# First mixer of a diffusion trunk: weights' low parts by adding DMAs, the out projection in halves, 9 convolution taps a step

## The chip, the core and the metric

The kernel runs on one core of a Trainium2 chip as a single program. The metric is the time of the device in microseconds (us), measured around the whole program; the kernel before has a median of 1498.23 us of three runs (1498.07 to 1499.12). The core has TensorE (matmul), VectorE (DVE in the profile), ScalarE (ACT), GpSimd (POOL) and SyncE (SP), which here only issues the DMAs of the weights. All engines run their own instruction lists in order and wait for each other by semaphores.

## What is computed

A trunk of two layers works on 384 tokens (256 latent, 128 context) of 1024 channels, in float32. Each layer is a half-step SwiGLU FFN, a mixer and another half-step FFN, each behind an RMS norm with shift, scale and gate from a condition vector. The mixer of layer 0 is the one that is changed. Cut to what matters, it is:

```
cq, ckv, kr, u = split(h @ w_in)                 # 384, 256, 32 and 1024 columns
q   = rms_norm(cq) @ w_qu ;  k, v = from rms_norm(ckv) @ w_kvu and kr
attn = softmax(q k^T / sqrt(96)) v               # 8 heads, 512 channels together
a, b = split(u)
g = depthwise_conv(a * sigmoid(b), w_dw) + b_dw  # 31 taps, 512 channels
g = silu(layer_norm(g) * g_ln + b_ln)            # the layer-norm goes over the 512 channels
out = concat([attn, g]) @ w_out                  # 1024 -> 1024
x = x + gate * out
```

## The kernel before

Everything is held transposed: channels on the 128 partitions, tokens along the free dimension. A float32 matmul is done as three matmuls of a rounded type (float32r): each operand is split into a high part (the value rounded) and a low part (the value minus its high part), and `mm3` (line 263; its three matmuls are lines 265 to 267) adds low x high, high x low and high x high into one bank of PSUM. Activations are split as they are made. Weights are split as they are used: `Step` is one tile of weights (128 x up to 2048 columns, 1 MB) with the work that uses it, and `stream` runs a list of steps. It loads raw tiles through a ring of three buffers on SP's queue, splits the tiles of this step and the next (`split`, line 193; its cast is line 202, its subtraction line 203: for each half of 1024 columns ScalarE casts to `whi`, VectorE subtracts to `wlo`; four buffers of each kind), calls the step's matmuls (`mm`), and the step's `post` after the next split. A raw buffer is loaded again when both halves are split.

The program's order is not an engine's order. The framework's planner orders each engine's list when the program is built: of what is ready by its own estimates, the earliest in the program goes first, so later work that is ready fills gaps. Semaphore waits hold the actual order to the data.

The mixer of layer 0 (`mixer_a`) has ten steps: seven tiles of `w_in` (`in_unit`, 48 matmuls of 386 columns each, in the order ORD), then query weights, key/value weights, query weights. Behind every tile that completes a group of 128 convolution channels, `taps` puts 31 taps of that group into background queues (`self.bg`); a tap is one multiply-add of VectorE over 128 x 399 (line 859; the first of each group is line 856). After each step's `post`, `pop_bg(BG1)` issues BG1 = 6 of them, alternating between two queues. Attention runs in four groups of two heads: scores of the next group, transposes and products of this one (`pv`), softmax of the next, and then `pop_bg(BG2)` with BG2 = 8. After the attention `pop_bg(1000)` issues all taps that are left. `conv_ln` makes the layer-norm over the 512 channels: sums over channels by matmuls with a matrix of constants (line 937), centring and squares, their sums (line 951), a reciprocal root by small VectorE steps, its broadcast by matmuls (line 437), then scaling, SiLU and the split into channels 4 to 7 of MXh and MXl. The out projection (`out_steps`) has four steps of 48 matmuls; each makes two of the eight output blocks from all eight channels, the attention's 0 to 3 and the convolution's 4 to 7. `mixer_a` ends with these lines:

```
rest(MXh, MXl)
self.Hh, self.Hl = self.take_h(F32R)
self.pop_bg(1000)
self.conv_ln(ub, acc, MXh, MXl)
self.stream(self.out_steps(a["woa"], MXh, MXl, lambda: self.mods[l, GM], nxt))
```

Of the kernel before, what the change touches and what calls it, by code (L numbers as in the profile page):

```python
# [43 lines left out]
LATE = 400  # L44

ORD = (0, 1, 4, 5, 2, 6, 3)
BG1, BG2 = 6, 8

V_GF1, V_GMIX, V_GF2, V_GFIN, V_BMOD, V_C = 0, 16, 32, 48, 56, 200
V_GQL, V_GKVL, V_BDW, V_GLN, V_BLN, V_WDW, V_GQH, V_GKH = 216, 219, 221, 225, 229, 233, 357, 358  # L50
# [9 lines left out]
def pair_col(i, k):  # L60

    return (k // 4 * 8 + i * 4 + k % 4) * P


class Step:
    def __init__(self, ap=None, cols=0, split=True, mm=None, post=None, ring="raw"):
        self.ap, self.cols, self.split, self.mm, self.post, self.ring = ap, cols, split, mm, post, ring
        self.raw = self.buf = None
        self.parts = []
        self.pos = 1000  # L70
        self.then = None
# [8 lines left out]
class Trunk:  # L80
# [79 lines left out]
    def stream(self, steps):  # L160
        depth = {"raw": NRAW, "rawm": NRAWM}
        lead = sorted([s for s in steps if s.ap is not None and s.pos < 1000], key=lambda s: s.pos)
        rest = {r: deque(s for s in steps if s.ap is not None and s.ring == r and s.pos == 1000) for r in depth}
        out = {r: deque() for r in depth}

        def load():
            def one(s):
                if len(out[s.ring]) == depth[s.ring]:
                    return False
                pool = self.rawp if s.ring == "raw" else self.ffnp  # L170
                s.raw = pool.tile([P, UN], F32, tag=s.ring, name=s.ring, bufs=depth[s.ring])
                self.nc.sync.dma_start(out=s.raw[:, :s.cols], in_=s.ap)
                out[s.ring].append(s)
                if s.then:
                    s.then()
                return True

            while lead and one(lead[0]):
                lead.pop(0)
            if lead:  # L180
                return
            for r in ("raw", "rawm"):
                if r == "rawm" and i + 4 < mod1:
                    continue
                while rest[r] and one(rest[r][0]):
                    rest[r].popleft()

        i = 0
        mod1 = min([k for k, s in enumerate(steps) if s.ring == "rawm" and s.pos == 1000], default=0)
        load()  # L190
        done_split = set()

        def split(s):
            half = UN // 2 if s.cols == UN else (s.cols // P + 1) // 2 * P
            for c0, c1 in ((0, half), (half, s.cols)):
                n = c1 - c0
                if s.buf:
                    hi, lo = (b[:, c0:c1] for b in s.buf)
                else:
                    hi, lo = (self.splitp.tile([P, UN // 2], F32R, tag=t, name="w" + t)[:, :n] for t in ("hi", "lo"))  # L200
                raw = s.raw[:, c0:c1]
                self.nc.scalar.copy(hi, raw)  # L202
                self.nc.vector.tensor_tensor(out=lo, in0=raw, in1=hi.bitcast(F32), op=ALU.subtract)  # L203
                s.parts.append((c0, c1, hi, lo))
            done_split.add(id(s))

        consumed = set()

        def retire():
            for q in out.values():  # L210
                while q and id(q[0]) in consumed:
                    q.popleft()
            load()

        lead0 = any(s.buf for s in steps)
        prev = None
        for i, s in enumerate(steps):
            want = 0
            for x in steps[i:]:
                if x.ap is not None and x.split:  # L220
                    if id(x) not in done_split:
                        if x.raw is None:
                            break
                        split(x)
                        consumed.add(id(x))
                        retire()
                    want += 1
                    if want == (3 if i < NLEAD and lead0 else 2):
                        break
            if prev is not None and prev.post:  # L230
                prev.post()
            if s.mm:
                s.mm(s)
            while self.mid:
                self.mid.pop(0)()
            if s.ap is not None and not s.split:
                consumed.add(id(s))
            retire()
            due, self.later = self.later, []
            for f in due:  # L240
                f()
            prev = s
        if prev is not None and prev.post:
            prev.post()
        while self.later:
            due, self.later = self.later, []
            for f in due:
                f()
# [315 lines left out]
            self.stream(steps)  # L564


    def in_unit(self, ap, posts, get=None, before=None, after=None):

        st = {}

        def mm(s):
            if before:
                before()
            ps = [(get or self.ps_mm)() for _ in posts]
            st["p"] = ps
            for k in range(ND):
                for i, p in enumerate(ps):
                    self.mm3(p[:, :TB], *s.w(pair_col(i, k)), self.Hh[:, k], self.Hl[:, k],
                             k == 0, k == ND - 1)
                if k == 4:  # L580
                    self.pop_mid()

            if after:
                after()

        def post():
            for f, p in zip(posts, st["p"]):
                f(p)

        return Step(ap, UN, True, mm, post)  # L590

    def norm_in(self, ps, out):

# [121 lines left out]
    def out_steps(self, w, MXh, MXl, gate, nxt):  # L715
# [17 lines left out]

        return [step(u) for u in range(ND // 2)]


    def mixer_a(self, l, nxt):
        nc, a, tc = self.nc, self.a, self.tc
        with tc.tile_pool(name="ma", bufs=1, reuse_waits="tile") as mp:
# [7 lines left out]
            with tc.tile_pool(name="map", bufs=1, reuse_waits="tile") as pp:  # L747
# [116 lines left out]
                def q_step(u):  # L864
# [4 lines left out]
                                self.mm3(p[:, :T], *s.w((3 * h + k) * P), cqh[:, k], cql[:, k], k == 0, k == 2)  # L869
                            nc.vector.tensor_tensor(out=qT[4 * u + h], in0=p[:, :T], in1=ropeq[:, h % 2], op=ALU.mult)  # L870

                    return Step(a["wqu"][u], 1536, True, mm)

                def kv_step():
                    st = {}
# [14 lines left out]
                                         k == 0, k == 1)  # L890
                            nc.scalar.copy(Vt[:, kt], p)

                    return Step(a["wkvu"], UN, True, mm)

                heads = []
                for h in range(8):
# [5 lines left out]
                def bg(s):  # L902
                    post = s.post

                    def f():
                        if post:
# [2 lines left out]
                    s.post = f  # L909
                    return s  # L910

                steps = [self.in_unit(w[j], [p_ua(j), p_ub(j)]) for j in range(4)]
                steps += [self.in_unit(w[4], [p_ckv(0), p_ckv(1)]),
                          self.in_unit(w[5], [p_kr, p_cq(0)]),
                          self.in_unit(w[6], [p_cq(1), p_cq(2)])]
                steps = [steps[i] for i in ORD]
                steps += [q_step(0), kv_step(), q_step(1)]
                self.stream([bg(s) for s in steps])
            with tc.tile_pool(name="maa", bufs=1, reuse_waits="tile") as ap:
# [2 lines left out]
                rest(MXh, MXl)  # L922
                self.Hh, self.Hl = self.take_h(F32R)
                self.pop_bg(1000)
                self.conv_ln(ub, acc, MXh, MXl)
                self.stream(self.out_steps(a["woa"], MXh, MXl, lambda: self.mods[l, GM], nxt))

    def conv_ln(self, ub, acc, MXh, MXl):
        nc = self.nc
        cols = ((0, TL), (271, 399))  # L930
        n = self.tb("sq", 399)
        nc.vector.tensor_tensor(out=n, in0=acc[0], in1=acc[1], op=ALU.add)
        some = [n, acc[2], acc[3]]
        p = self.ps_ax()
        for o, (c0, c1) in ((0, cols[0]), (TL, cols[1])):
            for j in range(3):
                nc.tensor.matmul(p[:, o:o + c1 - c0], lhsT=self.ones, rhs=some[j][:, c0:c1], start=(j == 0), stop=(j == 2))
        sq = []
        for j in range(4):
            for o, (c0, c1) in ((0, cols[0]), (TL, cols[1])):  # L940
                nc.vector.scalar_tensor_tensor(out=acc[j][:, c0:c1], in0=p[:, o:o + c1 - c0], scalar=-2.0,
                                               in1=acc[j][:, c0:c1], op0=ALU.mult, op1=ALU.add)
            s = ub[j][:, 0:399]
            nc.scalar.activation(s, acc[j], AF.Square)
            sq.append(s)
            if j % 2:
                nc.vector.tensor_tensor(out=sq[j - 1], in0=sq[j - 1], in1=s, op=ALU.add)
        p = self.ps_ax()
        for t, c in enumerate((0, P, 271)):
            for j in (0, 2):  # L950
                nc.tensor.matmul(p[:, t:t + 1], lhsT=sq[j][:, c:c + P], rhs=self.one, start=(j == 0), stop=(j == 2))
        r3 = self.tb("r3", 3)
        self.rsqrt(r3, p[:, 0:3], 1.0 / 512)
        nc.scalar.activation(self.tb("ba", 2), r3[:, 0:2], AF.Silu)
        r = self.spread(None, r3)
        for j in range(4):
            n = self.tb("ta")
            for o, (c0, c1) in ((0, cols[0]), (TL, cols[1])):
                nc.vector.tensor_tensor(out=n[:, o:o + c1 - c0], in0=acc[j][:, c0:c1], in1=r[:, o:o + c1 - c0],
                                        op=ALU.mult)  # L960
            g = self.tb("g")
            nc.scalar.activation(g, n, AF.Silu, scale=self.v(V_GLN + j), bias=self.v(V_BLN + j))
            self.split_to(MXh[:, 4 + j], MXl[:, 4 + j], g)


    def mixer_c(self, l, nxt):
# [286 lines left out]
```

## Time and profile before

| | |
|---|---|
| median of three runs | 1498.23 us |
| the profiled execution | 1496.57 us, span 1494.8 us |
| TensorE busy | 1441.5 us (96%) |
| VectorE busy | 1209.1 us (81%) |
| ScalarE busy | 641.1 us (43%) |
| DMA queues, all | 248.36 MB, mean 166 GB/s |

The span runs from the first to the last instruction. Times in the trace are microseconds from its start. Matmuls overlap, so the duration of one is longer than the step from one to the next. The first mixer lies between 309 and 497 us.

### The profile page before, as it was taken

To read this page: it belongs to the slowest core of one execution; us is meant where nothing else is said; L and a number is where in the kernel's file an instruction comes from. 1 tells how busy PE (TensorE), PEld (TensorE's weight loads), DVE (VectorE), ACT (ScalarE), POOL (GpSimd) and SP (SyncE) were. 2 spreads that over 40 slices of the span, in tenths; PEclk is the share of its full clock that TensorE was granted. 3 is DMA by queue.
4 is the path that set the end of the run, shared out by engine and by line. 5 is a ranking of instruction groups with operands and counts; after the bars stand their busy time and mean duration, and the time that the engine had idled before them with its cause. 6 is when DMAs were issued, how large, how long until landed. Compare 5 with 4: busy or idle time off the path is not lost.

```text
span 1494.8 us, 21749 instructions
## 1 busy us (share of the span) xinstructions
PE 1441.5 (96%) x8274; PEld 1397.9 (94%) x8274; DVE 1209.1 (81%) x2544; ACT 641.1 (43%) x1143; POOL 1.8 (0%) x8
## 2 busy tenths in 40 slices
PE   7999999999938999999999999999999999999997
PEld 5999999999827999999999999999985899999997
DVE  6999999979997999999959998544799689555443
ACT  4433443346633543333334333333477553433332
POOL 0000000000000000000000000000000000000000
PEclk8999999999978999999999999999999999999999
DMA  8656557643102566656655664243420155332331
GB/s 360 253 205 228 215 210 233 233 164 103 57 1 88 222 220 231 225 193 224 241 218 196 221 230 150 89 136 134 162 85 29 57 201 194 113 134 95 116 123 56
DMA packets 40168, 248.36 MB, mean 166 GB/s; under 512 B 4448, under 2 KB 6272, under 8 KB 16384
## 3 DMA queue, kind: packets, MB, share of 16 engines
q1 hardware_dynamic: 37728, 245.04, 45.5%
q10 hardware_dynamic: 2336, 1.94, 0.4%
q8 instruction: 65, 1.06, 0.3%
q14 instruction: 39, 0.32, 0.1%
HBM read 244.98 MB, written 1.98 MB: 165 GB/s over the span
## 4 chain that ended last, share of the span: by engine, by line
PE 94%; DVE 3%; ACT 2%; DMA 1%; issue 1%; SPq 0%; DVEq 0%; ACTq 0%
PE ps_mm L265 28%; PE ps_mm L266 28%; PE ps_mm L267 28%; PE ps_mm L637 2%; PE ps_ax L687 2%; DVE acc L859 1%; PE ps_tr L267 1%; PE ps_tr L265 1%; PE ps_tr L266 1%; DMA raw<-wm 1%; PE ps_tr L679 1%; PE ps_tr L675 0%; ACT pr L656 0%; PE ps_ax L288 0%; PE ps_ax L437 0%
## 5 line engine op out<-in xcount | busy, mean ns | idle before, releaser
L202 ACT CAST whi<-raw 128x1024 fp32r<-128x1024 f32 (+1 forms) x348 | 330.1, 950 | 647.7 <-PE ps_mm L267 566.4
L265 PE MATMUL ps_mm<-Hh,wlo 128*128 128x386 f32 x1568 | 533.0, 341 | 4.8 <-DVE wlo L203 3.9
L266 PE MATMUL ps_mm<-Hl,whi 128*128 128x386 f32 x1568 | 532.0, 339 | 0.6 <-DVE Hl L392 0.6
L267 PE MATMUL ps_mm<-Hh,whi 128*128 128x386 f32 x1568 | 530.9, 339 | 0.0
L203 DVE TENSOR_TENSOR wlo<-raw,whi 128x1024 fp32r<-128x1024 f32 (+1 forms) x348 | 381.8, 1098 | 164.5 <-ACT whi L202 162.1
L265 PEld LDWEIGHTS ps_mm<-Hh,wlo 128*128 128x128 f32 x1568 | 295.9, 189 | 7.4 <-DVE wlo L203 4.4
L266 PEld LDWEIGHTS ps_mm<-Hl,whi 128*128 128x128 f32 x1568 | 296.7, 189 | 2.1 <-DVE Hl L392 1.1
L267 PEld LDWEIGHTS ps_mm<-Hh,whi 128*128 128x128 f32 x1568 | 295.7, 189 | 0.0
L266 PE MATMUL ps_mm<-Gl,whi 128*128 128x384 f32 x704 | 236.7, 336 | 0.0
L265 PE MATMUL ps_mm<-Gh,wlo 128*128 128x384 f32 x704 | 236.7, 336 | 0.0
L267 PE MATMUL ps_mm<-Gh,whi 128*128 128x384 f32 x704 | 236.7, 336 | 0.0
L368 DVE SCALAR_TENSOR_TENSOR junk<-rawm,eb 128x1024 bf16<-128x1024 f32 x130 | 158.5, 1219 | 1.0 <-ACT eb L143 1.0
L368 DVE SCALAR_TENSOR_TENSOR rawm<-rawm,eb 128x1024 f32<-128x1024 f32 x130 | 158.5, 1219 | 0.3
L265 PEld LDWEIGHTS ps_mm<-Gh,wlo 128*128 128x128 f32 x704 | 132.0, 187 | 0.0
L267 PEld LDWEIGHTS ps_mm<-Gh,whi 128*128 128x128 f32 x704 | 132.0, 187 | 0.0
L266 PEld LDWEIGHTS ps_mm<-Gl,whi 128*128 128x128 f32 x704 | 132.0, 187 | 0.0
L519 ACT CAST Gh<-g 128x384 fp32r<-128x384 f32 x88 | 45.0, 512 | 84.9 <-DVE g L516 84.6
L509 ACT ACTIVATE sa<-ta,ba 128x256 f32<-128x256 f32 (+1 forms) x176 | 70.3, 447 | 5.2 <-DVE ta L506 5.0
L859 DVE SCALAR_TENSOR_TENSOR acc<-ub,vec,acc 128x399 f32<-128x399 f32 x120 | 69.8, 630 | 0.0
L516 DVE SCALAR_TENSOR_TENSOR g<-t,bb,sa 128x256 f32<-128x256 f32 (+1 forms) x176 | 65.3, 412 | 0.8 <-ACT sa L509 0.8
L520 DVE TENSOR_TENSOR Gl<-g,Gh 128x384 fp32r<-128x384 f32 x88 | 48.9, 555 | 12.2 <-ACT Gh L519 12.2
L460 DVE SCALAR_TENSOR_TENSOR X<-ps_mm,mod,X 128x256 f32<-128x256 f32 x88 | 32.5, 412 | 30.4 <-PE ps_mm L267 30.4
(270 smaller groups left out, 1240.5 us busy)
## 6 DMA issues: line engine op xcount, KB each, us to landing
raw<-wi SPq DMA_DIRECT2D x86, 1024.0 KB, 4.8
rawm<-wmt SPq DMA_DIRECT2D x64, 1024.0 KB, 4.8
raw<-wo SPq DMA_DIRECT2D x64, 704.0 KB, 4.1
raw<-wia SPq DMA_DIRECT2D x7, 1024.0 KB, 4.7
raw<-wm SPq DMA_DIRECT2D x6, 1024.0 KB, 8.9
raw<-wic SPq DMA_DIRECT2D x6, 1024.0 KB, 4.8
raw<-woa SPq DMA_DIRECT2D x4, 1024.0 KB, 4.8
raw<-woc SPq DMA_DIRECT2D x4, 1024.0 KB, 4.8
```

The lines of the kernel that those rows point to most:

```text
L202: self.nc.scalar.copy(hi, raw)
L203: self.nc.vector.tensor_tensor(out=lo, in0=raw, in1=hi.bitcast(F32), op=ALU.subtract)
L265: mm(out, lhsT=lo, rhs=rh, start=start, stop=False)
L266: mm(out, lhsT=hi, rhs=rl, start=False, stop=False)
L267: mm(out, lhsT=hi, rhs=rh, start=False, stop=stop)
L368: self.nc.vector.scalar_tensor_tensor(out=junk, in0=raw[:, i], scalar=1.0, in1=self.eb[:, c], op0=ALU.mult, op1=ALU.mult, accum_out=out[:, ...
L460: nc.vector.scalar_tensor_tensor(out=self.X[:, d, s0:s1], in0=ps[:, s0:s1], scalar=gate[:, d, c:c + 1], in1=self.X[:, d, s0:s1], op0=ALU.m ...
L509: nc.scalar.activation(sa[:, s0:s1], ta[:, s0:s1], AF.Silu, bias=ba[:, c:c + 1])
L516: nc.vector.scalar_tensor_tensor(out=g[:, s0:s1], in0=t2[:, s0:s1], scalar=bb[:, c:c + 1], in1=sa[:, s0:s1], op0=ALU.add, op1=ALU.mult)
L519: nc.scalar.copy(Gh[:, f], g)
L520: nc.vector.tensor_tensor(out=Gl[:, f], in0=g, in1=Gh[:, f].bitcast(F32), op=ALU.subtract)
L859: nc.vector.scalar_tensor_tensor(out=acc[j], in0=src(t), scalar=w(t), in1=acc[j], op0=ALU.mult, op1=ALU.add)
```

## The change

The subtraction that makes a weight's low part is replaced, for all weights of the first mixer, by a negated copy on ScalarE (which rounds, so it is the negative high part) and a DMA from GpSimd's queue that adds the raw weight to it in SBUF:

```diff
                 raw = s.raw[:, c0:c1]
                 self.nc.scalar.copy(hi, raw)
-                self.nc.vector.tensor_tensor(out=lo, in0=raw, in1=hi.bitcast(F32), op=ALU.subtract)
+                if s.add:
+                    self.nc.scalar.activation(lo, raw, AF.Copy, scale=-1.0)
+                    self.nc.gpsimd.dma_start(out=lo.bitcast(F32), in_=raw, accum_op=ALU.add)
+                else:
+                    self.nc.vector.tensor_tensor(out=lo, in0=raw, in1=hi.bitcast(F32), op=ALU.subtract)
```

A step of 1024 columns is split in one piece. Nine taps are issued after every step and every attention group:

```diff
-BG1, BG2 = 6, 8
+BG1, BG2 = 9, 9
```

The out projection's first three steps are cut into a half for channels 0 to 3 and a half for channels 4 to 7, which add into the same banks of PSUM; each half loads its own 512 KB. The layer-norm becomes three parts that stand between the first halves, and `last` is the fourth step, whole:

```diff
+    def out_halves(self, w, MXh, MXl, gate, nxt):
+        half = UN // 2
+        sts = [{} for _ in range(3)]
+        def step(u, h):
+            st = sts[u]
+            def mm(s):
+                if h == 0:
+                    get = self.ps_tr if u == 2 else self.ps_mm
+                    st["p"] = [get(), get()]
+                for k in range(4 * h, 4 * h + 4):
+                    for i, p in enumerate(st["p"]):
+                        self.mm3(p[:, :T], *s.w(pair_col(i, k) - h * half), MXh[:, k], MXl[:, k],
+                                 k == 0, k == ND - 1)
...
+            return Step(w[u][:, h * half:h * half + half], half, True, mm, post if h else None, add=True)
+        last = self.out_steps(w, MXh, MXl, gate, nxt)[3]
+        last.add = True
+        return [step(u, 0) for u in range(3)], [step(u, 1) for u in range(3)], last
...
-                self.conv_ln(ub, acc, MXh, MXl)
-                self.stream(self.out_steps(a["woa"], MXh, MXl, lambda: self.mods[l, GM], nxt))
+                ln = [Step(mm=lambda s, f=f: f()) for f in self.conv_ln(ub, acc, MXh, MXl)]
+                first, second, last = self.out_halves(a["woa"], MXh, MXl, lambda: self.mods[l, GM], nxt)
+                self.stream([x for p in zip(first, ln) for x in p] + second + [last])
```

`conv_ln` now returns `centre` (channel sums, centring, squares), `scale` (sums of squares, reciprocal root) and `finish` (broadcast, scaling, SiLU, split). The operations are the old ones, but for one: the four channel groups go into the first sums separately, where two of them were added on VectorE before:

```diff
-        n = self.tb("sq", 399)
-        nc.vector.tensor_tensor(out=n, in0=acc[0], in1=acc[1], op=ALU.add)
-        some = [n, acc[2], acc[3]]
...
+                for j in range(4):
+                    nc.tensor.matmul(p[:, o:o + c1 - c0], lhsT=self.ones, rhs=acc[j][:, c0:c1],
+                                     start=(j == 0), stop=(j == 3))
```

## Rows read from the trace of the kernel before

**Rows 1.** The page: busy time of an engine, share of the span, instructions.

```profile
PE 1441.5 (96%) x8274; PEld 1397.9 (94%) x8274; DVE 1209.1 (81%) x2544; ACT 641.1 (43%) x1143; POOL 1.8 (0%) x8
```

**Rows 2.** Waits of TensorE: waiter, whom for, total us, times, longest.

```profile
PE ps_ax L937 <- DVE sq L932: 19.2, 1, 19.2
```

**Rows 3.** Busy time by stretch: length, engines, clock, DMA share, GB/s.

```profile
315.00:385.00 70.00, 70.00 (x400) 68.41 (x399) 63.53 (x148) 37.19 (x61) 0.00 (x0) 1.00 0.33 115
385.00:433.40 48.40, 40.72 (x226) 31.01 (x225) 45.21 (x132) 33.91 (x89) 0.00 (x0) 0.93 0.07 23
433.40:452.00 18.60, 0.02 (x1) 0.05 (x1) 18.60 (x35) 0.00 (x0) 0.00 (x0) 0.55 0.00 0
452.00:489.00 37.00, 33.20 (x175) 31.77 (x176) 28.85 (x73) 17.50 (x31) 0.00 (x0) 0.91 0.32 114
```

The columns between length and clock are PE, PEld, DVE, ACT and POOL, with instruction counts.

**Rows 4.** VectorE in order of time: start, duration, line, operation, count.

```profile
427.98 3.90 DVE L859 SCALAR_TENSOR_TENSOR acc<-ub,vec,acc 128x399 f32<-128x399 f32 x7
...
433.83 17.51 DVE L859 SCALAR_TENSOR_TENSOR acc<-ub,vec,acc 128x399 f32<-128x399 f32 x32
451.25 0.58 DVE L932 TENSOR_TENSOR sq<-acc,acc 128x399 f32<-128x399 f32 x1
...
452.28 1.23 DVE L203 TENSOR_TENSOR wlo<-raw,whi 128x1024 fp32r<-128x1024 f32 x1
...
459.14 0.64 DVE L859 SCALAR_TENSOR_TENSOR acc<-ub,vec,acc 128x399 f32<-128x399 f32 x1
...
471.26 1.23 DVE L203 TENSOR_TENSOR wlo<-raw,whi 128x1024 fp32r<-128x1024 f32 x1 [0.32 <-ACT whi L202]
```

**Rows 5.** VectorE's groups by shape, 315 to 452 us: busy us, mean ns.

```profile
L203 DVE TENSOR_TENSOR wlo<-raw,whi 128x1024 fp32r<-128x1024 f32 x12 | 14.7, 1222 | 0.7 <-ACT whi L202 0.5
L661 DVE TENSOR_SCALAR Hh<-Hh,sm 128x384 f32<-128x384 f32 x12 | 4.8, 418 | 0.0
L203 DVE TENSOR_TENSOR wlo<-raw,whi 128x768 fp32r<-128x768 f32 x4 | 3.7, 955 | 0.3 <-ACT whi L202 0.3
...
L661 DVE TENSOR_SCALAR Hh<-Hh,sm 128x128 f32<-128x128 f32 x6 | 1.7, 284 | 0.0
```

**Rows 6.** TensorE in order of time, matmuls alone.

```profile
309.63 0.33 PE L265 MATMUL ps_mm<-Hh,wlo 128*128 128x386 f32 x1
...
371.56 0.34 PE L267 MATMUL ps_mm<-Hh,whi 128*128 128x386 f32 x1
...
474.81 0.44 PE L265 MATMUL ps_mm<-MXh,wlo 128*128 128x384 f32 x1 [2.88 <-ACT MXh L603]
...
497.13 0.33 PE L267 MATMUL ps_mm<-MXh,whi 128*128 128x384 f32 x1
497.30 0.34 PE L265 MATMUL ps_mm<-Hh,wlo 128*128 128x386 f32 x1
```

**Rows 7.** The chain that ended last: start, length, what.

```profile
460.19 1.10 PE ps_ax L937 x8
```

**Rows 8.** ScalarE in order of time.

```profile
301.49 1.05 ACT L202 CAST whi<-raw 128x1024 fp32r<-128x1024 f32 x1 [1.28 <-issue]
...
357.92 1.05 ACT L202 CAST whi<-raw 128x1024 fp32r<-128x1024 f32 x1
...
394.61 2.04 ACT L202 CAST whi<-raw 128x1024 fp32r<-128x1024 f32 x2
...
470.19 1.04 ACT L202 CAST whi<-raw 128x1024 fp32r<-128x1024 f32 x1 [4.11 <-issue]
```

**Rows 9.** DMA issues: out, in, count, KB each, median us to landing.

```profile
raw<-wi SPq DMA_DIRECT2D x86, 1024.0 KB, 4.8
...
raw<-wo SPq DMA_DIRECT2D x64, 704.0 KB, 4.1
...
rawm<-wm SPq DMA_DIRECT2D x2, 1024.0 KB, 10.0
```

**Rows 10.** GpSimd in order of time.

```profile
309.68 1.64 POOL L760 MEMSET ub<- 128x429 f32 x4 [309.24 <-PE ps_mm L266]
```

More of the change, by code (lines that the diff above doesn't have):

```diff
@@ L65, with __init__ @@
 class Step:
-    def __init__(self, ap=None, cols=0, split=True, mm=None, post=None, ring="raw"):
+    def __init__(self, ap=None, cols=0, split=True, mm=None, post=None, ring="raw", add=False):
         self.ap, self.cols, self.split, self.mm, self.post, self.ring = ap, cols, split, mm, post, ring
+        self.add = add
         self.raw = self.buf = None
@@ L193, in split @@
         def split(s):
-            half = UN // 2 if s.cols == UN else (s.cols // P + 1) // 2 * P
+            half = UN // 2 if s.cols in (UN, UN // 2) else (s.cols // P + 1) // 2 * P
             for c0, c1 in ((0, half), (half, s.cols)):
+                if c0 == c1:
+                    continue
                 n = c1 - c0
@@ L564, in ffn, with in_unit @@
             self.stream(steps)
-    def in_unit(self, ap, posts, get=None, before=None, after=None):
+    def in_unit(self, ap, posts, get=None, before=None, after=None, add=False):
         st = {}
@@ L588, in post @@
                 f(p)
-        return Step(ap, UN, True, mm, post)
+        return Step(ap, UN, True, mm, post, add=add)
     def norm_in(self, ps, out):
@@ L734, in out_steps, with post @@
         return [step(u) for u in range(ND // 2)]
+    def out_halves(self, w, MXh, MXl, gate, nxt):
[11 more added lines that the diff above has]
+                                 k == 0, k == ND - 1)
+            def post():
+                for i, p in enumerate(st["p"]):
+                    self.resid(2 * u + i, p, gate(), nxt)
+            return Step(w[u][:, h * half:h * half + half], half, True, mm, post if h else None, add=True)
+        last = self.out_steps(w, MXh, MXl, gate, nxt)[3]
+        last.add = True
+        return [step(u, 0) for u in range(3)], [step(u, 1) for u in range(3)], last
     def mixer_a(self, l, nxt):
@@ L870, in mm @@
                             nc.vector.tensor_tensor(out=qT[4 * u + h], in0=p[:, :T], in1=ropeq[:, h % 2], op=ALU.mult)
-                    return Step(a["wqu"][u], 1536, True, mm)
+                    return Step(a["wqu"][u], 1536, True, mm, add=True)
                 def kv_step():
@@ L891, in mm @@
                             nc.scalar.copy(Vt[:, kt], p)
-                    return Step(a["wkvu"], UN, True, mm)
+                    return Step(a["wkvu"], UN, True, mm, add=True)
                 heads = []
@@ L910, in bg @@
                     return s
[L912 to L915, printed above, removed]
+                steps = [self.in_unit(w[j], [p_ua(j), p_ub(j)], add=True) for j in range(4)]
+                steps += [self.in_unit(w[4], [p_ckv(0), p_ckv(1)], add=True),
+                          self.in_unit(w[5], [p_kr, p_cq(0)], add=True),
+                          self.in_unit(w[6], [p_cq(1), p_cq(2)], add=True)]
                 steps = [steps[i] for i in ORD]
@@ L930, in conv_ln @@
         cols = ((0, TL), (271, 399))
-        n = self.tb("sq", 399)
-        nc.vector.tensor_tensor(out=n, in0=acc[0], in1=acc[1], op=ALU.add)
-        some = [n, acc[2], acc[3]]
[L934 to L939, printed above, removed]
-            for o, (c0, c1) in ((0, cols[0]), (TL, cols[1])):
[L941 to L963, printed above, removed]
+        sq, st = [], {}
@@ new lines, in centre @@
+        def centre():
+            p = self.ps_ax()
+            for o, (c0, c1) in ((0, cols[0]), (TL, cols[1])):
+                for j in range(4):
+                    nc.tensor.matmul(p[:, o:o + c1 - c0], lhsT=self.ones, rhs=acc[j][:, c0:c1],
+                                     start=(j == 0), stop=(j == 3))
+            for j in range(4):
+                for o, (c0, c1) in ((0, cols[0]), (TL, cols[1])):
+                    nc.vector.scalar_tensor_tensor(out=acc[j][:, c0:c1], in0=p[:, o:o + c1 - c0], scalar=-2.0,
+                                                   in1=acc[j][:, c0:c1], op0=ALU.mult, op1=ALU.add)
+                s = ub[j][:, 0:399]
+                nc.scalar.activation(s, acc[j], AF.Square)
+                sq.append(s)
+                if j % 2:
+                    nc.vector.tensor_tensor(out=sq[j - 1], in0=sq[j - 1], in1=s, op=ALU.add)
@@ new lines, in scale, with finish @@
+        def scale():
+            p = self.ps_ax()
+            for t, c in enumerate((0, P, 271)):
+                for j in (0, 2):
+                    nc.tensor.matmul(p[:, t:t + 1], lhsT=sq[j][:, c:c + P], rhs=self.one, start=(j == 0), stop=(j == 2))
+            r3 = st["r"] = self.tb("r3", 3)
+            self.rsqrt(r3, p[:, 0:3], 1.0 / 512)
+            nc.scalar.activation(self.tb("ba", 2), r3[:, 0:2], AF.Silu)
+        def finish():
+            r = self.spread(None, st["r"])
+            for j in range(4):
+                n = self.tb("ta")
+                for o, (c0, c1) in ((0, cols[0]), (TL, cols[1])):
+                    nc.vector.tensor_tensor(out=n[:, o:o + c1 - c0], in0=acc[j][:, c0:c1], in1=r[:, o:o + c1 - c0],
+                                            op=ALU.mult)
+                g = self.tb("g")
+                nc.scalar.activation(g, n, AF.Silu, scale=self.v(V_GLN + j), bias=self.v(V_BLN + j))
+                self.split_to(MXh[:, 4 + j], MXl[:, 4 + j], g)
@@ L966, in mixer_c @@
+        return centre, scale, finish
     def mixer_c(self, l, nxt):
```

## The prediction

> **What bounds the kernel now.** I read the page first. TensorE is busy 96% of the span, VectorE 81% [rows 1], so a gain has to come out of the few places where TensorE stands still. TensorE's waits, longest in total first, begin with one of 19.2 us for VectorE's `sq` (line 932) [rows 2]. It lies inside the first mixer. A table by stage shows what goes on there [rows 3]: in 315 to 385 us (projections) TensorE has no gap and VectorE is busy 63.5 of 70; in 385 to 433.4 (attention) TensorE 40.7 and VectorE 45.2 of 48.4; in 433.4 to 452 TensorE runs nothing and VectorE is busy all 18.6; in 452 to 489 TensorE works again. VectorE's own sequence tells why [rows 4]: from 433.83 it runs 32 convolution taps back to back (17.51 us), then the layer-norm's first sum, then the low parts of the out projection's weights (wlo, the first at 452.28) with the last six taps between them, until 459.14 + 0.64 = 459.8. The out projection needs those low parts, the layer-norm the last tap. So this stage is bound by VectorE's backlog of taps, and the end of the mixer by the last tap plus the layer-norm's chain. ScalarE is busy 37.2, 33.9, 0 and 17.5 us in the four stretches [rows 3].
>
> **Low parts by DMA: what VectorE loses.** Between 315 and 452 us VectorE makes the low parts of 12 halves of 1024 columns and 4 of 768, 14.7 + 3.7 us busy [rows 5], all of them ahead of the last softmax. Neighbours in the sequence overlap by some 0.08 us, so they occupy about 12 x 1.14 + 4 x 0.87 = 17.2 us. All of it goes. The out projection's go too; one (471.26, 1.23 us) stands in the layer-norm's chain [rows 4].
>
> **9 taps a step.** There are ten steps and four attention groups: 60 + 32 = 92 of 124 taps before, 90 + 36 = 126 after, so none is left for behind the attention. A tap in a run costs 17.51 / 32 = 0.547 us [rows 4]. In the order of the program 60 + 16 = 76 taps stand ahead of the last softmax's end now, 90 + 18 = 108 then: 32 x 0.547 = 17.5 us more, against 17.2 us of low parts gone. VectorE thus gets through the last softmax about 0.3 us later; the taps that now follow it at 427.98 start at 428.3. Then come 124 - 108 = 16 taps, 8.8 us, and the last head pair's split among them (under 0.6; a subtraction of 768 columns takes 0.95 [rows 5]). The last tap ends near 437.6 instead of 459.8.
>
> **Out projection in halves.** Its first halves need channels 0 to 3 (attention) and weights whose low parts no longer wait for VectorE. TensorE can start at 433.9, when the last pair is split, perhaps a little sooner on the pairs before it. A half is 24 matmuls at 0.174 us (497.13 to 497.30 is one step) [rows 6], 4.2 us; the first ends at 438.1, just behind the last tap. Then the layer-norm's sums: 16 matmuls where there were 12, since the addition of two channels on VectorE (0.58 us) is dropped; the old last block of eight takes 1.10 us [rows 7], so 16 take 2.2, the last block beginning at 439.2. From that block to the first matmul on new channels the old trace has 474.81 - 460.19 = 14.6 us [rows 6, 7]: 453.8. Meanwhile TensorE has the second and third first halves, 8.4 us, and small sums and broadcasts (2.2 counted, 2.2 more): 450.9. It waits 2.9 us; the old one waited 2.88 at the same place [rows 6]. The rest, three second halves and the last unit, is 120 matmuls, as it was: 497.30 - 474.81 = 22.5 us, slow start included. The next FFN's first matmul comes at 453.8 + 22.5 = 476.3 instead of 497.3. Gain 21.0 us.
>
> **What is added.** (a) ScalarE writes each half twice. The cast takes 1.05 us [rows 8], the negated copy I take at the same (bounds 0.95 and 1.22, VectorE's pieces of 768 and 1024 columns [rows 5]). 28 of them are 29 us on an engine with some 85 us free in the four stretches; they hurt only inside a chain. In the attention up to four fall between the exponentials: at worst 4.2 us, at best nothing; I take 1.0. In the layer-norm's chain the pairs for the second halves come in, and VectorE's 1.23 us go out: I take 0, between -2.3 (that piece and the cast at 470.19 [rows 8] both gone) and +5.3 (five more copies in line).
>
> (b) The adding DMA. The trace holds no such transfer. Its time from issue to landing is bounded by the plain loads: 4.1 us for 704 KB, 4.8 for 1024 KB, 10.0 where loads stood in line at the start [rows 9]. The slope is 0.7 us for 320 KB, so 512 KB moved once gives 3.7 us, the lower end; the upper end is 10.0; I take 4.8, the row for 1 MB, since an add reads 512 KB twice. Where is that late? In the steady run of projections a buffer comes free one and a half units (12.6 us) ahead of its use; less two ScalarE pieces, 10.5 us are left. Two places are tighter. First unit: cast at 301.49, copy done at 303.6, needed at 309.63: 6.0 us. Last unit, second half: cast at 357.92 with ScalarE behind and two extra copies ahead of it, ready at 362.1; needed 24 matmuls before the last, which ends near 371.7, at 367.5: 5.4 us [rows 6, 8]. At 4.8 both hold; at 10.0 they cost 4.0 + 4.6 = 8.6 us. I put in 1.0 for both.
> The Trainium skill (DMA: Bandwidth & Descriptors, Anatomy of one DMA) has a fit for DMAs issued from GpSimd, 2.0 us plus the bytes at 436 GB/s, which is an estimate of 3.2 us for 512 KB; by it the 1.0 would be 0.
>
> (c) GpSimd's queue. An add waits there for ScalarE's copy and holds the adds behind it, which need later copies anyway. The four memsets of `ub` wait for the FFN's buffers until 309.68 and end at 311.3 [rows 10]. If the first unit's add stood behind them, it would land at 316 and cost 6.5 us once; the planner puts what is ready first ahead (the out projection's first casts, at 394.61, run before anything behind the attention [rows 8]), so I cost it at nothing. Without it the 6.5 us are inside the range.
>
> (d) Raw buffers come free when the add has landed, some 5 us later than now. Loads go out on SP three buffers ahead and take 4.8 us against some 8.7 us a unit: covered until adds land after about 13 us.
>
> **Sum.** -21.0 + 1.0 (attention) + 1.0 (landing) = -19.0. The profiled execution took 1496.57 us (the span of 1494.8 and 1.8 around it), 1.7 less than the median of 1498.23. 1496.57 - 19.0 = 1477.6, against the median 1479. Its own range: best -21.0 - 2.3 in the chain - 2.9 of waiting, 1472; worst -21.0 + 4.2 + 5, 1486.
>
> **Rivals.** *Slower: the adds can't keep pace.* From 309 to 372 us a half is used up every 4.2 us. If adds run one after another and each takes D us, the loss is 14 x (D - 4.2) in the projections, 4 x (0.75 D - 3.1) in the query weights (18 matmuls a half) and 4 x (D - 4.2) in the out projection (four of its eight halves are ready beforehand): 21 D - 88. It eats the 19.0 at D = 5.1; at D = 6 it is 38 us, time 1498 + 19 = 1517. For it: an add reads two operands and writes one, weights come at 115 GB/s beside it [rows 3], and loads in line took 10.0 us. Against it: the slope of the loads prices 512 KB at 1.1 us, three passes at 3.4, under 4.2.
>
> *Less: the layer-norm's chain stretches.* ScalarE's pairs for the second halves fall between squares, SiLUs and casts (5.3 us), those in the attention cost their 4.2: 1479 + 5.3 + 3.2, 1488. For it: ScalarE runs in order, and a weight cast stands in that chain already (470.19) [rows 8]. Against it: ScalarE is free for over half of that stretch.
>
> *The adds starve behind VectorE.* VectorE's normalisations (line 661) run at (418 - 284) / 256 = 0.52 ns an element, the subtraction at (1222 - 955) / 256 = 1.04 [rows 5], so the former use a faster mode. If GpSimd could do nothing during each, the ceiling is their whole time, 12 x 0.42 + 6 x 0.28 on `Hh` and a third of that on `Hl`: 9 us, 1488. For it: they sit where the out projection's adds are issued. Against it: those adds have most of the attention to land. The Trainium skill (SBUF — State Buffer, Who interferes with whom) has the rule behind this: a DMA issued from GpSimd can't get its descriptors written while VectorE holds both ports in a fast mode. By that rule an add is under 1 us late here; the trace agrees that line 661 runs twice as fast, and can't show the wait.
>
> *No change: landings near 10 us.* 8.6 us at the two tight places for the 1.0, and the stretched chain: 1488 + 7.6, 1496. Only loads in line speak for it.
>
> **How the numbers follow.** Forecast 0.55, stretched chain 0.20, starving 0.05, no change 0.06, slower 0.14. A measurement of this kernel tells 0.2%, 3 us, from no change. Faster 0.80, same 0.06, slower 0.14. The range 1470 to 1495 takes in the forecast, the stretched chain and starving: 0.80.
>
> **What would show it.** Right: TensorE's wait for `sq` gone and no run of taps without matmuls beside it; last tap near 438; first new-channel matmul near 454; the next FFN's first matmul near 476; line 203 missing from VectorE between 315 and 475; adds landing in 4 to 6 us, with no wait of TensorE above 1 us for one. Wrong: TensorE waiting for `wlo` at each half; adds of 6 us and more one behind another; a last tap after 445; more than 16 us from the layer-norm's last sums to the first new-channel matmul.

## The result, and the profile after

The changed kernel takes 1478.53 us (median of 4 runs, 1477.75 to 1478.81), the kernel before 1498.38 (4 runs): a ratio of 0.9863, 95% interval 0.9851 to 0.9875. The profiled execution took 1478.81 us, its span is 1477.0. By the medians 19.9 us were gained, by the two profiled executions (1496.57 before) 17.8; 19.0 were forecast.

The page after: engines' busy time, two DMA queues (packets, MB, share of 16 engines' span), and the new transfers (count, KB each, median us from issue to landing).

```profile
PE 1442.5 (98%) x8278; PEld 1397.7 (95%) x8278; DVE 1178.5 (80%) x2515; ACT 665.3 (45%) x1171; POOL 26.0 (2%) x36
...
q1 hardware_dynamic: 38160, 245.04, 46.0%
q0 software_dynamic: 4032, 14.16, 5.2%
...
wlo<-raw POOLq DMA_DIRECT2D x24, 512.0 KB, 6.8
```

TensorE does what it did before [rows 1] in a span shorter by 17.8 us; VectorE lost 31 us of work, ScalarE gained 24. Where the time came from stands in the table by stretch, beside [rows 3]:

```profile
315.00:385.00 70.00, 67.89 (x391) 66.51 (x390) 60.92 (x159) 50.98 (x75) 13.80 (x16) 1.00 0.97 233
385.00:433.40 48.40, 42.93 (x224) 31.96 (x223) 44.42 (x129) 36.12 (x83) 3.44 (x4) 0.97 0.47 122
433.40:452.00 18.60, 18.59 (x118) 17.14 (x117) 13.47 (x40) 8.92 (x21) 1.72 (x2) 0.99 0.44 108
452.00:489.00 37.00, 34.02 (x186) 33.24 (x185) 28.38 (x69) 24.23 (x44) 1.72 (x2) 0.95 0.67 213
```

In 433.4 to 452, where TensorE had 0.02 us of work, it now has 18.59. And in the first stretch the DMA engines' share rose from 0.33 to 0.97: that is what the adds cost, and it is paid in a resource that had stood idle for two thirds of that stretch. TensorE's waits, 300 to 500 us:

```profile
PE ps_mm L272 <- ACT Hh L663: 3.6, 1, 3.6
PE ps_mm L272 <- ACT MXh L610: 2.6, 1, 2.6
PE ps_mm L272 <- DMA wlo<-raw: 2.1, 2, 1.3
```

The 19.2 us for `sq` [rows 2] are gone; in their place stands nothing above 3.6. VectorE and TensorE after, in order of time (rows left out between; they answer to [rows 4] and [rows 6]):

```profile
433.77 3.60 DVE L893 SCALAR_TENSOR_TENSOR acc<-ub,vec,acc 128x399 f32<-128x399 f32 x6
...
440.78 2.63 DVE L893 SCALAR_TENSOR_TENSOR acc<-ub,vec,acc 128x399 f32<-128x399 f32 x4
```
```profile
365.55 0.41 PE L272 MATMUL ps_mm<-Hh,wlo 128*128 128x386 f32 x1 [0.75 <-DMA wlo<-raw]
...
383.18 0.51 PE L272 MATMUL ps_mm<-cath,wlo 128*128 128x512 f32 x1 [1.33 <-DMA wlo<-raw]
...
430.05 0.44 PE L272 MATMUL ps_mm<-MXh,wlo 128*128 128x384 f32 x1 [3.59 <-ACT Hh L663]
...
443.57 1.49 PE L973 MATMUL ps_ax<-acc,cst 128*128 128x256 f32 x10
...
456.65 0.97 PE L272 MATMUL ps_mm<-MXh,wlo 128*128 128x384 f32 x4 [2.63 <-ACT MXh L610]
...
479.13 0.34 PE L272 MATMUL ps_mm<-Hh,wlo 128*128 128x386 f32 x1
```

The last tap ends at 440.78 + 2.63 = 443.41 (before: 459.78), the layer-norm's last block of sums starts at 443.57 (460.19), the first matmul on new channels at 456.65 (474.81), the next FFN at 479.13 (497.30). The gain at the last tap is 16.4 us, and 18.2 at the FFN. The out projection's first halves begin at 430.05, in a gap of the attention.

### The profile page after: what moved, and what is told of

The parts are those of the page before. It is cut to its first block, busy times and chain, and to the rows that moved or that the text cites. A ratio compares the mean times of both kernels' runs of the same rounds, so it can differ in the third digit from the quotient of the medians.

```text
span 1477.0 us, 21867 instructions
## 1 busy us (share of the span) xinstructions
PE 1442.5 (98%) x8278; PEld 1397.7 (95%) x8278; DVE 1178.5 (80%) x2515; ACT 665.3 (45%) x1171; POOL 26.0 (2%) x36
## 3 DMA queue, kind: packets, MB, share of 16 engines
q8 instruction: 65, 1.06, 0.3%
## 5 line engine op out<-in xcount | busy, mean ns | idle before, releaser
L210 DVE TENSOR_TENSOR wlo<-raw,whi 128x1024 fp32r<-128x1024 f32 (+1 forms) x320 | 348.3, 1089 | 155.0 <-ACT whi L205 152.5
```

## Experiments

The theory: VectorE's work ahead of the last tap sets the end of the mixer, so the gain is what the adds take off VectorE; where the taps stand and how the out projection is cut only decide how much of it arrives. The rival: the 9 taps a step (or the halves) bring the gain by putting work beside TensorE's, and the adds only keep the projections from becoming late. A second pair: do the adds have room to spare on the DMA engines, or are they at their limit?

All ratios are against the kernel before on the same chip, whose median there was 1496.86 to 1498.38 us, so medians of two rows can differ by 1.5 us for that reason alone. The last three columns are us from the span's start in the profiled execution, which took up to 3.7 us more than the kernel's median (e8: 1485.16).

| kernel | median us | ratio, 95% | attention ends | last tap | next FFN |
|---|---|---|---|---|---|
| before | 1498.38 | | 432.81 | 459.78 | 497.30 |
| after | 1478.53 | 0.9863 (0.9851-0.9875) | 437.70 | 443.41 | 479.13 |
| e1 taps | 1499.44 | 1.0013 (1.0003-1.0022) | 451.69 | 461.43 | 500.11 |
| e3 halves | 1500.32 | 1.0015 (1.0005-1.0024) | 434.33 | 463.53 | 502.38 |
| e4 taps, halves | 1500.30 | 1.0014 (1.0005-1.0023) | 449.95 | 460.76 | 500.75 |
| e2 adds | 1482.56 | 0.9900 (0.9883-0.9916) | 435.04 | 445.68 | 483.17 |
| e6 adds, taps | 1481.86 | 0.9892 (0.9876-0.9909) | 440.61 | 446.33 | 483.50 |
| e5 adds, halves | 1486.06 | 0.9921 (0.9906-0.9936) | 438.10 | 448.74 | 486.20 |
| e8 all, 11 and 4 taps | 1481.47 | 0.9899 (0.9883-0.9914) | 448.84 | 445.68 | 485.53 |
| g1 adds in out projection only | 1492.71 | 0.9975 (0.9966-0.9985) | 454.02 | 459.31 | 496.21 |
| g2 adds in projections only | 1488.98 | 0.9942 (0.9927-0.9957) | 440.55 | 451.33 | 489.54 |
| f3 adds for one half of two | 1485.78 | 0.9921 (0.9906-0.9936) | 442.54 | 447.83 | 486.16 |
| f1 one tile by VectorE | 1483.10 | 0.9911 (0.9894-0.9927) | 443.36 | 449.08 | 483.24 |
| e7 half an add more each | 1495.26 | 0.9980 (0.9970-0.9989) | 454.26 | 459.98 | 496.71 |

### The three parts, alone and in pairs

**e1, 9 taps alone.** The kernel before with

```diff
-BG1, BG2 = 6, 8
+BG1, BG2 = 9, 9
```

> The kernel before with 9 taps a step and a group and nothing else. Theory (VectorE is short of time up to the last tap, so moving taps only moves the shortage): attention ends some 17 us later, the last tap stays near 460, time 1494 to 1502. Rival (it is the order of the taps alone): the wait for the sums goes, time near 1480.

Measured 1499.44, as the theory had it. The taps do move: only 7 start behind the attention, where 38 did. But the attention ends 18.9 us later and the last tap 1.65 later. What is put ahead of the attention delays it by its own length, since VectorE is short in both places.

**e3, halves alone.** The changed kernel with `BG1, BG2 = 6, 8` and

```diff
-                if s.add:
+                if False:
```

> Only the out projection in halves with the layer-norm's parts between, low parts by VectorE, 6 and 8 taps. Theory: the low parts still wait behind the taps and the planner had the first halves ahead of the layer-norm anyway: no change, 1496 to 1500. Rival (the order of the out projection carries part of the gain): 1488 to 1492.

Measured 1500.32. TensorE's longest wait of this kernel in 300 to 500 us:

```profile
PE ps_ax L973 <- DVE acc L893: 17.6, 2, 17.0
```

It is the 19.2 of [rows 2] under another name: TensorE waits for the taps of the third channel group all the same, and the halves put nothing in its place. Their low parts stand on VectorE behind the same 32 taps, and their first matmul comes at 454.05, when the wait is over.

**e4, both without adds**: e3's diff with 9 and 9.

> The changed kernel without the adding DMAs: 9 taps and halves, low parts by VectorE. Theory: no adds, no gain, 1494 to 1502, the attention ending near 450. Rival (the adds only hide work that is hidden anyway): 1478 to 1482.

Measured 1500.30; last tap 460.76. Both together gain nothing either.

**e2, adds alone**: 6 and 8 taps, and whole out-projection steps, with adds, behind the layer-norm:

```diff
-                ln = [Step(mm=lambda s, f=f: f()) for f in self.conv_ln(ub, acc, MXh, MXl)]
-                first, second, last = self.out_halves(a["woa"], MXh, MXl, lambda: self.mods[l, GM], nxt)
-                self.stream([x for p in zip(first, ln) for x in p] + second + [last])
+                for f in self.conv_ln(ub, acc, MXh, MXl):
+                    f()
+                steps = self.out_steps(a["woa"], MXh, MXl, lambda: self.mods[l, GM], nxt)
+                for s in steps:
+                    s.add = True
+                self.stream(steps)
```

> Low parts of all first-mixer weights by adding DMAs, but 6 and 8 taps and whole steps in the out projection (the layer-norm with the four groups summed by matmuls). Theory: VectorE has 17 us less ahead of the attention's end and the out projection's low parts come without it, but 32 taps still stand behind the attention in the program: last tap near 449, time 1484 to 1490. Rival (the freed time on VectorE is all that matters, since the planner pulls ready taps forward): 1478 to 1481. Rival (the adds cost what they save): 1496 to 1500.

Measured 1482.56: 15.6 of the 19.9 us without the other two parts, a time between the ranges of the theory and of the first rival. And without more taps a step 69 taps start before 385 us, where the kernel before has 43 and the changed one 70. The taps had been held back by VectorE's work, not by the number 6.

**e5, adds and halves** (the changed kernel with 6 and 8 taps), and **e6, adds and taps** (the changed kernel with e2's tail).

> The changed kernel with 6 and 8 taps again (adds and halves). Theory after the first four runs (the adds free VectorE, and the planner pulls ready taps into the room: 69 taps before 385 us with 6 a step, 71 with 9): close to the changed kernel, 1479 to 1482. Rival (9 a step is what sets the taps early): 1484 to 1488.

> The changed kernel with the out projection in whole steps behind the layer-norm (adds and 9 taps). Theory (the halves carry what the adds alone lack, as the small parts of the layer-norm stand in line with the matmuls): 1481 to 1484. Rival (the taps carry it, the planner pulls the first halves forward anyway): 1478 to 1480.

Measured 1486.06 and 1481.86 (e6's four runs from 1478.45 to 1483.12): e5 missed its theory and fell into the rival's range, e6 kept to its theory's. With the adds in, 9 taps are worth 7.5 us where the out projection is in halves (1486.06 to 1478.53) and nothing clear of the spread where it is whole (1482.56 to 1481.86). The halves cost 3.5 us at 6 taps. At 9 they seem to gain 3.3, but that lies within e6's own spread, and 2.9 of the 4.4 us by which e6's profiled execution (1483.02) is later at the next FFN are there at the last tap already, behind a wait of 3.0 us for one add at the key/value weights (1.33 in the changed kernel).

Where e5 loses its time shows in ScalarE in order of time, and in TensorE's longest wait (300 to 500 us):

```profile
415.48 1.04 ACT L205 CAST whi<-raw 128x1024 fp32r<-128x1024 f32 x1 [6.04 <-DMA raw<-woa]
416.43 1.05 ACT L207 ACTIVATE wlo<-raw 128x1024 fp32r<-128x1024 f32 x1
```
```profile
PE ps_tr L686 <- ACT Hl L684: 6.0, 1, 6.0
```

A cast of the out projection's weights, drawn into the attention, waits 6.04 us for its load, and the softmax copies stand behind it on ScalarE. The attention ends at 438.1 with 16 taps still to come behind it; in the changed kernel it ends at 437.7 with 7. Nine taps at 0.547 us [rows 4] are 4.9 us, with the later end 5.3, and the last tap is 5.3 later. So the 7.5 us are in the main the price of one cast in a bad place, which the order built with 9 taps doesn't have; that the number 9 gains anything by itself is not shown.

### Which adds carry it

**g1**: `add=True` taken from the projections, query and key/value weights. **g2**: taken from the out projection.

> The changed kernel with adds for the out projection alone; projections, query and key weights split by VectorE. Theory (the 17 us that VectorE is spared ahead of the attention's end are the gain): attention ends near 450 as without adds, the first halves run into it, 1492 to 1497. Rival (the gain comes from the out projection's low parts no longer waiting behind the taps): 1480 to 1484.

> The changed kernel with adds for projections, query and key weights, the out projection's low parts by VectorE. Theory: attention ends near 438 and the last tap comes near 444 as in the changed kernel; the first halves wait for low parts made among the last taps, and three or four such pieces of 1.2 us fall into the layer-norm's chain: 1480 to 1484. Rival as in the run before: 1492 and more.

Measured 1492.71 and 1488.98. Against 1496.86 for the kernel before on that chip, g1 gains 4.2 us, g2 7.9, both together (the changed kernel) 19.9. Neither alone is enough: in g1 the last tap is where it was (459.31). In g2 it is 451.33, where the theory had 444 and 1480 to 1484 us, and so missed by 5: five of the out projection's low parts, VectorE's again, stand among the last taps (437.21 to 448.18).

**f3, half the adds**: the first half of each tile of 2048 columns goes back to VectorE. **f1**: the last projection tile alone goes back.

```diff
-                if s.add:
+                if s.add and (c0 or s.cols != UN):
```
```diff
+                steps[6].add = False
```

> The changed kernel with adds for one half in two of the 2048-column tiles, the other half by VectorE (eight pieces, 9.1 us ahead of the attention). Theory: the DMA engines' share in the projections falls from 0.97 to some 0.7 and no wait for an add is left, but VectorE is short again: last tap near 452, 1484 to 1489. Rival (the full rings cost more than they spare): 1474 to 1477.

> The changed kernel with the low parts of the last projection tile by VectorE. Theory: TensorE's 2.1 us of waiting for adds there go, VectorE has 2.3 us more ahead of the attention: 1476 to 1480, within 2 us of the changed kernel. Rival (waits for adds are what makes the attention late): 1474 to 1476.

Measured 1485.78, in the theory's range, and 1483.10, above both of f1's. f3 in 315 to 385 us:

```profile
315.00:385.00 70.00, 69.60 (x399) 68.17 (x398) 62.33 (x155) 45.20 (x69) 8.60 (x10) 1.00 0.74 190
```

The DMA share falls from 0.97 to 0.74 and no wait for an add is left; it is slower all the same, since VectorE has its pieces back (last tap 447.83). f1 was meant to buy the 2.1 us of waits for two subtractions, but only 0.75 of them stand at that tile (365.55). Both waits do go, and a new one takes their place as TensorE's longest (the second is 3.1 for `Hh`):

```profile
PE ps_ax L694 <- ACT Hl L684: 4.7, 1, 4.7
```
```profile
408.72 1.04 ACT L205 CAST whi<-raw 128x1024 fp32r<-128x1024 f32 x1 [3.90 <-DMA raw<-woa]
409.67 0.47 ACT L688 COPY Hl<-ps_tr 128x384 f32<-128x384 f32 x1
410.04 0.59 ACT L684 COPY Hl<-ps_ax 128x512 f32<-128x512 f32 x1
```

It is e5's stall again: a cast of the out projection's weights waits 3.90 us for its load, with softmax copies behind it on ScalarE. The attention ends 5.7 us later than in the changed kernel. What the rest of that is, and why the order that the planner writes out has the cast there, was not told apart.

### How near the DMA engines' limit

**e7, half an add more**: behind each add of the six later projection units, twelve in all, a second one of 512 columns into a scratch tile. (The expectation names the query and key weights too; the edit leaves them as they are.)

```diff
+                    if getattr(s, "twice", False):
+                        self.turn += 1
+                        self.nc.gpsimd.dma_start(out=self.scr[self.turn % 3], in_=raw[:, :UN // 4], accum_op=ALU.add)
...
+                for q in steps[1:]:
+                    q.twice = True
```

> The changed kernel with a second add of half the size behind each add from the second projection tile to the query weights' end, into a scratch tile that nothing reads. Theory (an add takes 2.7 us of all DMA engines, which with the loads' 1.3 is 4.0 of the 4.2 us that a half lasts; the rings have no room left): 1.4 us more per half, 5.4 against 4.2, over 13 halves and the query and key weights some 15 to 20 us slower than the changed kernel, 1493 to 1500, TensorE waiting for wlo. Rival (busy rings, but adds only queue for each other): within 4 us of the changed kernel, 1477 to 1483.

Measured 1495.26: 16.7 us of the 19.9 gone. Its longest wait, and 315 to 385 us:

```profile
PE ps_mm L275 <- DMA wlo<-raw: 13.1, 6, 4.5
```
```profile
315.00:385.00 70.00, 58.06 (x302) 56.46 (x301) 45.81 (x116) 41.33 (x62) 19.81 (x23) 0.90 0.97 219
```

The DMA share is 0.97, as in the changed kernel; what gives is TensorE, 67.89 to 58.06. The query weights' first matmul comes at 390.91 instead of 374.66, 16.3 us late (17.4 counted from the first projection unit, which starts 1.1 earlier here). So the adds had next to no room left. The sum by which that follows stands in the next section.

**e8, 11 and 4 taps.** `BG1, BG2 = 11, 4`.

> The changed kernel with 11 taps a step and 4 a group. If VectorE's room lies in the projections and softmax suffers from taps put between: attention ends 2 to 4 us earlier, 1474 to 1477. If the planner already fills the room (theory of the first four runs): 1477 to 1480. If taps ahead of the projections' own work make TensorE wait there: 1480 to 1485.

Measured 1481.47, in the third range. No tap is left behind the attention, yet the attention itself ends at 448.84 (in the slowest of the four runs): more taps ahead only trade one for the other, as in e1. No version tried beats the changed kernel.

## Why the prediction was right, step by step

**The bound** was right: VectorE's backlog. Between 315 us and the last tap, before and after (the columns of [rows 3]):

```profile
315.00:459.78 144.78, 118.52 (x659) 106.80 (x658) 135.12 (x326) 71.88 (x150) 0.00 (x0) 0.91 0.21 71
```
```profile
315.00:443.41 128.41, 120.82 (x674) 107.22 (x672) 114.53 (x309) 92.15 (x172) 18.10 (x21) 0.99 0.71 174
```

VectorE's work fell by 135.12 - 114.53 = 20.6 us. The low parts of the projections, query and key/value weights, 17.2 by the prediction's count, the four of the out projection that stood ahead of the last tap, 4 x 1.14, and the sum of two channel groups, 0.5, make 22.3; other pieces, the taps most of all, took just under 2 longer. The last tap came only 16.4 sooner, because VectorE's idle time rose from 9.7 to 13.9 us. That is the mis-sized term: the prediction let VectorE go on without a gap and put the last tap at 437.6; it was 443.4. Of the 4.2 us of added idle time 3.1 lie before the scores begin (9.6 up to 388.06, before 6.5 up to 387.09).

**9 taps a step** was credited with the wrong part. The prediction counted taps per step, 32 more ahead of the last softmax's end. Behind the attention's end 38 taps start in the kernel before, 16 in e2 with 6 a step, 7 in the changed kernel: the freed time moved most of them, not the 9. Only with the halves do the 9 show (e5), and there mainly by where one cast fell.

**Out projection in halves**: the first halves run where they were put, even earlier (430.05 for 433.9). They save no time in themselves (e3). That they pay by filling TensorE while VectorE's chain runs is not shown: with whole steps and adds the planner starts the out projection as early (427.43 in e2, 432.35 in e6), and the difference to e6 lies within e6's spread.

**The layer-norm's chain** took 456.65 - 443.57 = 13.1 us from the last block of sums to the first new channel, 14.6 forecast; ScalarE's pairs were priced between -2.3 and +5.3, and it is -1.5. So the rival of a stretched chain (0.20) did not come. From there to the next FFN 22.5 us, as worked out.

**Attention.** 1.0 us was allowed for ScalarE's copies; the attention ends 4.9 later than before. 1.3 of it is there when the first unit starts (310.89 for 309.63), which e1 and e3 have too, without adds; 2.1 are the waits for adds. The rest, 1.5, stands in the attention itself, where TensorE waits 3.6 for `Hh` at 430.05. What goes before that on VectorE and ScalarE:

```profile
423.29 3.35 DVE L893 SCALAR_TENSOR_TENSOR acc<-ub,vec,acc 128x399 f32<-128x399 f32 x6
427.01 0.56 DVE L611 TENSOR_TENSOR MXl<-ps_ax,MXh 128x384 fp32r<-128x384 f32 x1 [0.37 <-ACT MXh L610]
427.48 1.21 DVE L659 TENSOR_REDUCE mx<-ps_mm 128x1 f32<-128x384 f32 x3
```
```profile
428.80 0.67 ACT L663 ACTIVATE Hh<-ps_mm,mx,rs 128x384 f32<-128x384 f32 x1 [1.82 <-DVE mx L661]
```

The scores are done at 422.81, but VectorE runs six taps and a split ahead of their row maxima, and ScalarE stands idle for 1.82 us until these are there. So the wait is made by taps, not by a copy on ScalarE, for which the 1.0 was set aside. The kernel before waits there too (3.2 and 1.7 us, for `Hh` and `Hl`), so how the 1.5 us come about is not told in full.

**The adds.** ScalarE's copy takes 1.06 us as assumed. Of the wait of 2.1 (1.0 taken) 0.75 stands at the last projection unit, one of the two tight places named, and 1.33 at the key/value weights (383.18), whose two adds the prediction left out of its list of tight places and of the rival's sum. The 0.75 is no slow landing: ScalarE's negated copy came late there, and GpSimd waited 12.46 us for it before it issued the add at 360.87 (the row stands below). The landing, 4.8 taken, was 4.7 where the DMA engines had room and 9.1 beside loads. DMA in 309 to 345 us of the changed kernel, and in 433 to 475:

```profile
q0 software_dynamic: 1244, 4.51, 67.2%
q1 hardware_dynamic: 486, 3.59, 27.9%
...
wlo<-raw POOLq DMA_DIRECT2D x9, 512.0 KB, 9.1
raw<-wia SPq DMA_DIRECT2D x4, 1024.0 KB, 9.1
```
```profile
wlo<-raw POOLq DMA_DIRECT2D x4, 512.0 KB, 4.7
```

The Trainium skill (DMA: Bandwidth & Descriptors, Anatomy of one DMA) gives by its fit an estimate of 3.2 us for 512 KB issued from GpSimd; no group of such adds in this trace landed in under 4.7 (median), so the measurement decides.

**The slower rival**, adds that can't keep pace, had the right mechanism and a wrong measure of it. It asked for adds one after another, each over 5.1 us; landings were 9.1 and cost little, because adds were issued every 4.2 us all the same (322.16 to 347.55), so that two or more were under way at once. What counts is the engines' time. One add takes 5.2% x 1477 / 27 = 2.8 us of all 16 engines (28 adds are 27 of 512 KB), one load of 1024 KB (1.05 MB) 0.279 x 36 / 3.59 x 1.05 = 2.9, so 1.5 per half. Together 4.3 us, and a half is used up every 4.2. It held with nothing to spare; e7, which adds 1.4 us twelve times (16.8), paid 16.3. With adds half as large again in six of the seven projection units 2.8 us of the gain are left (e7).

**GpSimd.** An add's issue took 0.86 us (the first 1.00):

```profile
303.74 1.00 POOL L208 DMA_DIRECT2D wlo<-raw  x1 [303.30 <-ACT wlo L207]
...
310.95 1.64 POOL L794 MEMSET ub<- 128x429 f32 x4 [0.61 <-PE ps_mm L273]
...
360.87 0.86 POOL L208 DMA_DIRECT2D wlo<-raw  x1 [12.46 <-ACT wlo L207]
```

The first unit's adds went ahead of the memsets, as argued, so the 6.5 us were not due. The starving rival was not put to the test: the four issues in the attention (400.29, 403.62, 405.51 and 414.49, each 0.86) fall beside none of VectorE's normalisations, which run from 394.55 to 397.61 and from 409.73 to 413.79 around them.

**The signs** named beforehand mostly held, but three did not: the last tap (443.4, not near 438), the landing (6.8 us in the median of the 24 adds of 512 KB, not 4 to 6) and the longest wait for an add (1.3 us, not under 1).

**The total** came out nearer than its terms, and that is luck in part. The last block of sums began 4.4 us later than forecast (443.57 for 439.2), the chain was 1.5 shorter, and the 2.0 us set aside for attention and landing had covered most of the rest: 476.3 + 4.4 - 1.5 = 479.2, forecast 476.3 + 2.0 = 478.3, measured 479.13.

## What to carry to other kernels

Where one engine's total of work ahead of a point sets the time, taking work off it is the gain, and moving its work about gives nothing: here the two reorderings lost 1 to 2 us each without the adds and together gave 4 with them. Before work is handed to the DMA engines, sum what one unit costs of all 16 and set that against the time in which a unit is used up, rather than a single transfer's landing. Test the parts of a change in all their combinations, since a part that is worth nothing alone may be worth 7.5 us, or cost 3.5, beside another; and look in the trace for what made the difference, which here was one cast that waited for its load among the softmax's copies.

## What the hardware showed that was not expected

An adding DMA of 512 KB from SBUF to SBUF takes about as much of the DMA engines as a load of 1024 KB (2.8 and 2.9 us of all 16). Beside such adds the loads take twice as long to land: 9.1 us in 309 to 345 against 4.7 there before.

```profile
raw<-wia SPq DMA_DIRECT2D x3, 1024.0 KB, 4.7
```
